# A hybrid MLA and forgetting-attention block: the load of the rotary queries moved behind the mask biases in the sync queue, and half of the first rotary stores moved one stage later

## The chip, the cores and the metric

The kernel runs on one core of a Trainium2 chip. The metric is the device time of one execution in microseconds; lower is better. Three executions of the kernel before gave 579.85 us as the median (579.05 to 580.62).

A core has a matrix engine (TensorE: PE, and PEld for its weight loads), VectorE (DVE), ScalarE (ACT), GpSimd (POOL) and a sync engine (SP). In this kernel every DMA is issued by SP. SP takes its instructions one after the other, so a DMA that has to wait for something keeps all later ones waiting behind it.

## The reference

One decoder layer on 512 real tokens and 16 learned tokens ahead of them, model width 1024. A combined projection of the normalised input feeds two attention branches of 16 heads each and the gates. MLA is the branch with low-rank queries and keys and rotary positions (scores have a 64-wide part and a 32-wide rotary part). FoX is the forgetting attention: its scores get a bias from cumulated log forget gates, one row per head.

```
(cq, ckv, k_pe_raw, z_mla, fq, fk, fv, f_logit, z_fox, gate_a, gate_b) = split(u @ w_in)
q  = rmsnorm(cq) @ w_uq      # per head: 64 plain + 32 rotary columns
kv = rmsnorm(ckv) @ w_ukv    # per head: 64 key + 64 value columns
o_mla = softmax(causal(q_m k_m^T * MLA_SCALE)) v_mla             # q_m, k_m = plain part and rope(rotary part)
o_fox = softmax(causal(fq fk^T * FOX_SCALE + cum_t - cum_s)) fv  # cum = cumsum(log_sigmoid(f_logit + b))
mixed = (sigmoid(gate_a) * ((o_mla * silu(z_mla)) @ w_br_mla)
       + sigmoid(gate_b) * ((o_fox * silu(z_fox)) @ w_br_fox)) @ w_out
out = x + rmsnorm(mixed)
```

Only the 512 real tokens are returned.

## The kernel before

Everything is kept transposed: features on the 128 partitions, tokens along the free dimension. Products are made in parts (a high and a low half of weights and activations, three matmuls for one), so that TensorE's fast types give nearly float32 results.

**Stages.** Attention runs in 16 stages, two heads (a pair) each: `stages = [(br, pr) ...]` with `br` 1 for FoX, 0 for MLA, and `pr` the pair. Stage 0 is FoX pair 0, stage 1 MLA pair 0, stage 2 FoX pair 1, and so on; an even stage is FoX, an odd one MLA. The loop over `si` writes one stage as: `sc()`, the two heads' scores (`st`), their eviction by VectorE (L979: scale, add the bias, row minimum) and the exponentials on ScalarE; `late`, which is the last stage's `values` (`ov`: probabilities times values); then a `fill` of projections for the stages to come (`z`, `mq`, `mk`, `v` in an FoX stage; `fq`, `fk`, `v` in an MLA stage), with `n0` and `n1` in between, which normalise the probabilities into `pn` (L1050 on ScalarE, L1054 on VectorE, small pieces on GpSimd at L1035 to L1040) and send them through DMA transposes into `pt`, five in a stage (6, 10, 14, 10 and 8 tiles). So `ov` of stage n stands on TensorE right behind `st` of stage n+1, and needs the transposes of stage n. TensorE runs in the order in which the program is written (`manual_schedule`).

**Weights in stages.** The loads `wraw` are 512 KB pieces of `w_in`. ScalarE or VectorE finds their peak (`junk` L201, `sc` L203), a tiny matmul `scale` spreads it over the partitions, ScalarE makes the high half (L258), and GpSimd (L271, L272) or VectorE (L269) the low half. A buffer of `wraw` is free for the next load when its low half is made. In an MLA stage three of them are loaded, two for the gates `z` of the next FoX stage: their `scale` matmul stands in the middle of the `v` matmuls of that same MLA stage.

**Rotary queries.** They are made for eight heads at once (`pe_unit`), 0 to 7 in the beginning and 8 to 15 in stages 5 to 9, and stored to `qpe_dram` (`store`: two DMAs for one of the halves `x` = 0 or 1, from `gT0` or `gT1`). `load_qp(pr)` reads one pair's back as `QP`, 256 KB; the MLA scores of pair `pr` read `QP` (stage 2 pr + 1). `QP` has one buffer, free when the MLA scores of the pair before are done. The load is called in `q_done`, when the projection `mq` of stage 2 pr is written.

**Mask biases.** `bias(pr)` loads the two heads' rows of cumulated gates (`cbp`, 264 KB each) from `c_dram`; `masked_bias` makes the causal copy on GpSimd (`cbm`). Their buffers are free when VectorE has evicted the FoX scores.

**Order of SP's queue.** A scheduler sets it from the order in which the program is written, what each DMA depends on and its estimates of time; `tc.issue_after(ins)` puts what is written under it behind `ins` on the same engine, and `keep_in_program_order` holds the stores in the order written. The queue therefore need not follow the text.

Of the kernel before, what the change touches and what calls it, by code (L numbers as in the profile page):

```python
# [26 lines left out]
NH = 16  # L27
# [24 lines left out]
def f32(ap):  # L52
    return ap.bitcast(F32)
# [3 lines left out]
def block_kernel(ctx: ExitStack, tc: tile.TileContext, x, meta_tokens, pre_norm_g, w_in, fox_forget_b,  # L57
# [303 lines left out]
    def run(steps):  # L361
        for _, fn in steps:
            fn()
# [359 lines left out]
    with ExitStack() as att:  # L723
# [38 lines left out]
        nc.gpsimd.memset(vh[:, 0], 0.0)  # L762
        for b in range(4):
            nc.gpsimd.memset(pn[b // 3][:, PN_STEP * b % 15], 0.0)
        gT = []
        masks, normed, whole, turned_p, between = [], [], [], [], []

        wuqh = wuq.rearrange("p k (h e) -> p k h e", e=NOPE + ROPE)
# [1 line left out]
        def load_qp(pr):  # L770
            dma(f32(QP), qpe_dram[2 * pr : 2 * pr + 2].rearrange("h i x f s -> (h i x f) s"))

        def q_mla(pr):
            ld = []

            def load():
                if not ld:
                    ld.append(wload([wuq[:, :, 192 * pr : 192 * pr + 192], wukv[:, 256 * pr : 256 * pr + 256]], mla_room))

            def get():  # L780
                load()
                u, raw, _, _ = ld[0]
                wh, wl = half_rooms(u)
                cuts = [(raw[:, 0:384].rearrange("p (b e) -> p b e", e=96)[:, :, 0:NOPE], lambda t: t[:, 0:256].rearrange("p (b e) -> p b e", e=NOPE)),
                        (raw[:, 384:640].rearrange("p (h a e) -> p a h e", h=2, a=2), lambda t: t[:, 256:512].rearrange("p (a h e) -> p a h e", a=2, h=2))]
                for src, to in cuts:
                    with tc.issue_after(behind[0]) if behind else nullcontext():
                        nc.scalar.copy(to(wh), src)
                for src, to in cuts:
                    split_lo(nc.gpsimd, to(wl), src, to(wh))  # L790
                w = mw[pr] = [(wh[:, o : o + 128], wl[:, o : o + 128]) for o in range(0, 512, 128)]
                return (lambda k: w[k][0]), (lambda k: w[k][1])
            get.load = load

            halves = hl_done(("q", 0, pr), S, S)

            def q_done(i, ps):
                halves(i, ps)
                if pr:
                    load_qp(pr)  # L800
            return unit(f"mq{pr}", get, cq_act, 2, REAL, q_done)


# [289 lines left out]

            return scores, norm(0), norm(1), values

        def stores(a, b):

            written[0] = True
            for x in range(2):
                store0(x, a, b)  # L1100
            written[0] = False

        def bias(pr):

            return [nc.sync.dma_start(cb[0][h], c_dram[2 * pr + h : 2 * pr + h + 1].broadcast_to([128, L])).ins
                    for h in range(2)][1:]
# [33 lines left out]
        pe0, rest0, store0, both0 = pe_unit(0)  # L1140
# [41 lines left out]
        for si, (br, pr) in enumerate(stages):  # L1182
            last = si + 1 == len(stages)
# [66 lines left out]
        for si, (br, pr) in enumerate(stages):  # L1250
            last = si + 1 == len(stages)
            sc, n0, n1, va = attention(br, pr)

            fill = fills[si]
            sc()
            for fn in late:
                fn()
            if si == 0:
# [24 lines left out]
            else:  # L1283
# [2 lines left out]
                run(fill[:3])  # L1286
                if si == 3:
                    with tc.issue_after(turned_p[0]):
                        stores(4, 8)
                run(fill[3:5])  # L1290
                if si == 1:

# [1 line left out]
                if si == 2:  # L1294
                    behind.clear()
                n0()
                if pr and not (br or last):
                    bias(pr + 1)
                if br:
                    sets[si][0].scale()  # L1300
                for job in middles[si]:
# [22 lines left out]
                            peaks(sets[si + 1][1:2], nc.vector)  # L1324
                if not (br or last):
                    masked_bias()
                if 6 <= si < 8:

                    written[0] = True
                    rest1(si - 6)  # L1330
                    written[0] = False
# [382 lines left out]
```

## Time and profile before

| | |
|---|---|
| median of three executions | 579.85 us (579.05 to 580.62) |
| the profiled execution | 580.09 us |
| span of its instructions | 578.3 us |
| TensorE busy | 563.0 us, 97% of the span |
| VectorE, ScalarE, GpSimd busy | 467.3, 390.4, 232.0 us |
| DMA: moved, share of 16 engines' span | 97.74 MB, 71.8% |
| granted TensorE clock | 0.999 |

The profile tells of one execution. Its rows give, for each instruction or run of alike instructions, the start and the length in microseconds, the engine, the line and the tiles (out<-in); in square brackets stands how long the engine was idle before, and who ended that. On the queue of SP (`SPq`) a row is the issuing of DMAs, not the transfer. The chain of waits follows the last instruction back through what released it; there a row with DMA begins at the issue and ends when the data has landed.

### The profile page before, as it was taken

How to read it: one execution, taken by the hardware profiler on the slowest of the kernel's cores; microseconds unless marked ns; L12 is line 12 of the kernel's file. 1: busy time of each engine (PE TensorE's matmuls, PEld its weight loads, DVE VectorE, ACT ScalarE, POOL GpSimd, SP SyncE). 2: the span in 40 equal slices, each digit the busy share in tenths (PEclk: the TensorE clock that was granted, in tenths of full speed). 3: DMA queues.
4: the chain of work that ended last, by engine and by line, in shares of the span. 5: the costliest groups of instructions: out<-in, count | busy, mean ns of one | idle time of the engine just before them, and what ended most of it. 6: DMA issues, size and time to landing. Idle time of an engine off the chain costs nothing.

```text
span 578.3 us, 11369 instructions
## 1 busy us (share of the span) xinstructions
PE 563.0 (97%) x3864; PEld 401.1 (69%) x3864; DVE 467.3 (81%) x1251; ACT 390.4 (68%) x859; POOL 232.0 (40%) x346
## 2 busy tenths in 40 slices
PE   8999989999999999999999999999999999999995
PEld 7888657667668567667666676545686675788884
DVE  5868799878878989868878788879958986478966
ACT  6858688887895886877877878864443463343762
POOL 4331823775695597746837856600000000000000
PEclk9999999999999999999999999999999999999999
DMA  8425999889999897997999987659823230333603
GB/s 282 108 74 153 244 169 294 191 196 244 198 247 191 160 202 123 227 216 152 233 234 186 214 182 144 156 99 297 284 74 109 74 111 10 107 103 109 219 0 145
DMA packets 220537, 97.74 MB, mean 169 GB/s; under 512 B 131864, under 2 KB 210080, under 8 KB 220480
## 3 DMA queue, kind: packets, MB, share of 16 engines
q1 hardware_dynamic: 220480, 97.03, 71.8%
q8 instruction: 30, 0.49, 0.3%
q14 instruction: 27, 0.22, 0.1%
HBM read 62.62 MB, written 4.23 MB: 116 GB/s over the span
## 4 chain that ended last, share of the span: by engine, by line
PE 69%; DVE 9%; ACT 3%; DMA 2%; issue 1%; DVEq 0%; POOL 0%; ACTq 0%; POOLq 0%
PE z L104 15%; PE pg L104 10%; PE py L104 8%; PE x L104 6%; PE v L104 6%; PE st L104 5%; PE fk L104 5%; PE fq L104 5%; PE ov L104 4%; PE mq L104 2%; PE y L104 2%; DMA wraw<-in_w_in_dram 1%; DVE sc L203 1%; DVE w L269 1%; DVE wl L110 1%
## 5 line engine op out<-in xcount | busy, mean ns | idle before, releaser
L104 PEld LDWEIGHTS <-w 128*128 128x128 f16 x1584 | 149.9, 98 | 114.8 <-issue 3.9
L1014 ACT ACTIVATE sf<-sf,nb 128x272 f32<-128x272 f32 (+3 forms) x128 | 72.7, 569 | 25.3 <-DVE nb L979 23.1
L104 PE MATMUL z<-hTh,w 128*128 128x512 f16 x256 | 81.9, 380 | 0.0
L272 POOL TENSOR_TENSOR w<-wraw,w 128x1024 f16<-128x1024 f32 x35 | 74.9, 2141 | 2.3
L104 PE MATMUL pg<-hTh,w 128*128 128x512 f16 x240 | 72.6, 379 | 0.7 <-DVE w L269 0.7
L1054 DVE SCALAR_TENSOR_TENSOR pn<-sf,ri,pn 128x512 f16<-128x512 f32 (+3 forms) x128 | 70.8, 611 | 1.5 <-ACT pn L1050 1.5
L219 POOL TENSOR_SCALAR sc<-sc,su 128x2 f32<-128x2 f32 (+2 forms) x22 | 8.3, 378 | 147.4 <-DVE sc L216 147.4
L258 ACT ACTIVATE w<-wraw,sc 128x1024 f16<-128x1024 f32 x43 | 48.3, 1144 | 24.6 <-DVE sc L218 18.9
L1050 ACT ACTIVATE pn<-sf,ri 128x128 f16<-128x128 f32 (+3 forms) x128 | 59.5, 547 | 0.5 <-DVE ri L1020 0.5
L104 PE MATMUL z<-hTl,w 128*128 128x512 f16 x128 | 48.5, 379 | 0.0
L110 DVE TENSOR_TENSOR wl<-wraw,w 128x512 fp32r<-128x512 f32 (+1 forms) x44 | 38.5, 882 | 12.2 <-PE scale L104 4.4
L271 POOL TENSOR_SCALAR wraw<-wraw,sc 128x1024 f32<-128x1024 f32 x35 | 39.7, 1134 | 19.8 <-ACT w L258 19.8
L104 PE MATMUL pg<-hTl,w 128*128 128x512 f16 x120 | 45.5, 379 | 0.0
L104 PE MATMUL st<-hlk,hlq 64*128 64x272 f32 (+4 forms) x480 | 41.8, 299 | 0.3 <-DVE hlk L387 0.2
L104 PE MATMUL fk<-hTh,w 128*128 128x272 f16 (+1 forms) x224 | 40.1, 276 | 0.0
L104 PE MATMUL v<-hTh,w 128*128 128x272 f16 (+1 forms) x224 | 39.4, 276 | 0.0
L104 PEld LDWEIGHTS st<-hlk,hlq 64*128 64x128 f32 x480 | 33.1, 186 | 6.5 <-ACT vh L903 2.5
L104 PE MATMUL ov<-pt,vp 128*64 128x512 f16 (+4 forms) x416 | 32.7, 307 | 3.1 <-DMA pt<-pn 2.9
L104 PE MATMUL fq<-hTh,w 128*128 128x512 f16 x112 | 34.5, 380 | 0.0
L104 PEld LDWEIGHTS <-vp 128*64 128x64 f16 (+1 forms) x416 | 21.9, 109 | 16.0 <-issue 7.4
L1417 ACT CAST w<-wraw 128x512 fp32r<-128x512 f32 x28 | 16.8, 617 | 23.1 <-DVE wraw L1426 18.6
L165 ACT CAST w<-wraw 128x1024 fp32r<-128x1024 f32 (+1 forms) x20 | 20.2, 1014 | 17.0 <-PE py L104 15.3
(342 smaller groups left out, 1481.0 us busy)
## 6 DMA issues: line engine op xcount, KB each, us to landing
wraw<-in_w_in_dram SPq DMA_DIRECT2D x47, 512.0 KB
room<-in_w_in_dram SPq DMA_DIRECT2D x9, 512.0 KB
cbp<-c_dram SPq DMA_DIRECT2D x16, 264.0 KB
wraw<-in_w_br_fox_dram SPq DMA_DIRECT2D x8, 512.0 KB
tb<-in_w_out_dram SPq DMA_DIRECT2D x8, 512.0 KB
wraw<-in_w_br_mla_dram SPq DMA_DIRECT2D x8, 512.0 KB
wraw<-in_w_out_dram SPq DMA_DIRECT2D x6, 512.0 KB
QP<-qpe_dram SPq DMA_DIRECT2D x8, 256.0 KB
```

Source lines behind the costliest of these rows:

```text
L104: nc.tensor.matmul(*a, **k)
L110: return eng.tensor_tensor(out=lo, in0=src, in1=f32(hi), op=ALU.subtract)
L165: nc.scalar.copy(wh[:, :n], raw[:, :n])
L203: tc.keep_in_program_order(nc.vector.tensor_reduce(out=mp, in_=raw, op=ALU.max, axis=AX.X, apply_absolute_value=True))
L219: nc.gpsimd.tensor_scalar(out=r, in0=t, scalar1=su[:, 5:6], scalar2=1.0, op0=ALU.mult, op1=ALU.mult)
L258: self.hi = nc.scalar.activation(hi, raw, AF.Copy, scale=self.s).ins
L271: nc.gpsimd.tensor_scalar(out=raw, in0=raw, scalar1=self.s, scalar2=1.0, op0=ALU.mult, op1=ALU.mult)
L272: nc.gpsimd.tensor_tensor(out=lo, in0=raw, in1=hi, op=ALU.subtract)
L1014: exps[b // 3] = nc.scalar.activation(sf, sf, AF.Exp, bias=sums["nb"][:, h, b : b + 1], scale=-1.0, accum_out=sums["su"][:, h, b : b + 1]).ins
L1050: normed[:] = [nc.scalar.activation(hi, sf, AF.Copy, scale=rib).ins]
L1054: nc.vector.scalar_tensor_tensor(out=lo, in0=sf, scalar=rib, in1=hi, op0=ALU.mult, op1=ALU.subtract)
L1417: nc.scalar.copy(to[0], src)
```

## The change

Four edits. `q_done` issues the load of the rotary queries behind the second mask bias, where one was asked for in this stage. The mask biases of pair pr + 1 are asked for in the FoX stage of pair pr right behind its scores (pairs 1 to 6) and no longer in the MLA stage behind `n0`. `stores` writes one half `x`. In stage 3 the half x = 0 of the stores for heads 4 to 7 stays behind the transposes of stage 2, and the half x = 1 moves behind those of stage 3.

```diff
             def q_done(i, ps):
                 halves(i, ps)
                 if pr:
-                    load_qp(pr)
+                    with tc.issue_after(biased[0]) if biased else nullcontext():
+                        load_qp(pr)
+                    biased.clear()
...
-        def stores(a, b):
+        def stores(x, a, b):
 
             written[0] = True
-            for x in range(2):
-                store0(x, a, b)
+            store0(x, a, b)
             written[0] = False
...
             fill = fills[si]
             sc()
+            if br and 1 <= pr < NH // 2 - 1:
+                biased[:] = bias(pr + 1)
             for fn in late:
...
                 if si == 3:
                     with tc.issue_after(turned_p[0]):
-                        stores(4, 8)
+                        stores(0, 4, 8)
...
                 n0()
-                if pr and not (br or last):
-                    bias(pr + 1)
                 if br:
...
                 if not (br or last):
                     masked_bias()
+                if si == 3:
+                    with tc.issue_after(turned_p[0]):
+                        stores(1, 4, 8)
```

On TensorE, VectorE, ScalarE and GpSimd the order of the instructions stays as it was. On SP the mask biases keep their places too; six of the eight loads of `QP`, two stores and one weight load move.

SP's queue around the beginning of stage 8 (FoX pair 4), before. `gT_1000` is `gT1`, the source of the half x = 1; `wraw` are weight loads, `vp<-vh` the transpose of the values.

```order
L98 DMA_TRANSPOSE pt<-pn_757 128x8x128
L98 DMA qpe_dram<-gT_1000 2x16x512 x2
L98 DMA QP<-qpe_dram 128x512
L98 DMA wraw_4160<-in_w_in_dram 128x8x128
L98 DMA wraw_4162<-in_w_in_dram 128x8x128
L98 DMA_TRANSPOSE vp_761<-vh 128x9x128
L1105 DMA cbp_746<-c_dram 128x528
L1105 DMA cbp_745<-c_dram 128x528
L98 DMA_TRANSPOSE pt<-pn_756 128x6x128
```

The same place now:

```order
L98 DMA_TRANSPOSE pt<-pn_757 128x8x128
L98 DMA qpe_dram<-gT_1000 2x16x512 x2
L98 DMA wraw_4162<-in_w_in_dram 128x8x128
L98 DMA wraw_4164<-in_w_in_dram 128x8x128
L98 DMA_TRANSPOSE vp_761<-vh 128x9x128
L1106 DMA cbp_746<-c_dram 128x528
L1106 DMA cbp_745<-c_dram 128x528
L98 DMA QP<-qpe_dram 128x512
L98 DMA_TRANSPOSE pt<-pn_756 128x6x128
```

The load of `QP` passed two weight loads, one transpose of values and the two mask biases, and stands now right ahead of the stage's transposes of probabilities. Stage 10 changes in the same way, there behind two stores of 6x16x512. For pairs 1, 2, 3 and 6 (stages 2, 4, 6 and 12) the load comes from the stage before, where it stood ahead of the odd stage's transposes (for pair 1 ahead of one more weight load); those of pairs 0 and 7 stay.

SP's queue at the beginning of stage 3 (MLA pair 1), before:

```order
L98 DMA_TRANSPOSE pt<-pn_757 128x8x128
L98 DMA qpe_dram<-gT_999 4x16x512 x2
L98 DMA qpe_dram<-gT_1000 4x16x512 x2
L98 DMA wraw_1924<-in_w_in_dram 128x8x128
L98 DMA wraw_2195<-in_w_uq_dram 128x2x192
L98 DMA wraw_2195<-in_w_ukv_dram 128x256
L98 DMA wraw_2355<-in_w_in_dram 128x8x128
L98 DMA_TRANSPOSE vp_760<-vh 128x9x128
L98 DMA wraw_2357<-in_w_in_dram 128x8x128
L98 DMA QP<-qpe_dram 128x512
L98 DMA_TRANSPOSE pt<-pn_756 128x6x128
```

and now, from behind the two stores from `gT0` (`gT_999`) to the end of the stage:

```order
L98 DMA wraw_1922<-in_w_in_dram 128x8x128
L98 DMA wraw_2197<-in_w_uq_dram 128x2x192
L98 DMA wraw_2197<-in_w_ukv_dram 128x256
L98 DMA wraw_2357<-in_w_in_dram 128x8x128
L98 DMA wraw_2359<-in_w_in_dram 128x8x128
L98 DMA_TRANSPOSE vp_760<-vh 128x9x128
L98 DMA_TRANSPOSE pt<-pn_756 128x6x128
L98 DMA_TRANSPOSE pt<-pn_757 128x10x128
L98 DMA_TRANSPOSE pt<-pn_756 128x10x128
L98 DMA_TRANSPOSE pt<-pn_756 128x14x128
L98 DMA_TRANSPOSE pt<-pn_757 128x8x128
L98 DMA qpe_dram<-gT_1000 4x16x512 x2
```

The two stores from `gT1` and the load of `QP` left the place ahead of the transposes, and the second weight load stands now ahead of the values' transpose.

More of the change, by code (lines that the diff above doesn't have):

```diff
@@ L764, in block_kernel @@
             nc.gpsimd.memset(pn[b // 3][:, PN_STEP * b % 15], 0.0)
-        gT = []
+        gT, biased = [], []
         masks, normed, whole, turned_p, between = [], [], [], [], []
```

## The prediction

> **What bounds the kernel now.** I read the page first, then the busy times of four pairs of stages side by side, then TensorE in time where those differ, and last the queue of SP.
>
> ```profile
> span 578.3 us, 11369 instructions
> PE 563.0 (97%) x3864; PEld 401.1 (69%) x3864; DVE 467.3 (81%) x1251; ACT 390.4 (68%) x859; POOL 232.0 (40%) x346
> ```
>
> TensorE is busy for all but 15 us of the span. No matmul is removed by the change, so it can gain only where TensorE waits. The next view has the engines' busy time from one FoX `st` to the next, for stages 6+7, 8+9, 10+11 and 12+13 (length, then PE, PEld, DVE, ACT, POOL, granted clock, DMA share, GB/s).
>
> ```profile
> 186.79:225.94 39.15, 39.15 (x323) 26.74 (x322) 35.32 (x112) 30.96 (x73) 29.65 (x42) 1.00 0.89 173
> 225.94:266.33 40.39, 39.40 (x323) 27.00 (x322) 32.03 (x112) 31.04 (x73) 25.86 (x39) 1.00 0.96 197
> 266.33:307.07 40.74, 39.32 (x322) 26.95 (x322) 32.58 (x113) 31.42 (x74) 28.04 (x40) 1.00 1.00 204
> 307.07:346.23 39.16, 39.16 (x322) 26.75 (x322) 32.43 (x113) 31.28 (x73) 25.96 (x38) 1.00 0.93 197
> ```
>
> The four pairs do the same matmuls. Two take 39.15 and 39.16 us with TensorE busy throughout: that is the floor of a pair. Stages 8+9 take 1.23 us more (40.39 - 39.16), stages 10+11 1.58 us more (40.74 - 39.16). The granted clock is 1.00 in all. What TensorE waited for there, and once more in stage 4, the engine's rows in time tell:
>
> ```profile
> 144.55 2.26 PE L104 MATMUL st<-hlk,hlq 64*128 64x272 f32 x30
> 146.97 0.62 PE L104 MATMUL ov<-pt,vp 80*64 80x512 f16 x4 [0.16 <-PE st L104]
> 259.51 0.16 PE L104 MATMUL scale<-sc,spread 128*128 128x2 bf16 x1 [0.98 <-ACT junk L201]
> 288.82 2.13 PE L104 MATMUL ov<-pt,vp 80*64 80x512 f16 x26 [1.42 <-DMA pt<-pn]
> ```
>
> At 259.51 the spreading of the gates' peaks is late, since ScalarE's peak is late; at 288.82 the probabilities' transposes are late. Both come from SP's queue:
>
> ```profile
> 250.47 7.75 DMA wraw<-in_w_in_dram
> 284.55 4.19 DMA pt<-pn
> ```
>
> These are from the chain of waits: a weight load issued at 250.47 lands at 258.22, and a transpose issued at 284.55 lands at 288.74, 0.08 us ahead of the matmul. Now SP's queue ahead of them, with the wait that stands out in it and the DMA engines' share in that wait:
>
> ```profile
> 224.63 1.28 SPq L98 DMA_DIRECT2D qpe_dram<-gT  x2
> 230.05 0.35 SPq L98 DMA_DIRECT2D QP<-qpe_dram  x1
> 230.50 1.00 SPq L98 DMA_DIRECT2D wraw<-in_w_in_dram  x2
> ...
> 235.53 1.00 SPq L1105 DMA_DIRECT2D cbp<-c_dram  x2
> 236.63 9.64 SPq L98 DMA_TRANSPOSE pt<-pn  x5
> ...
> 248.01 5.54 SPq L98 DMA_DIRECT2D wraw<-in_w_in_dram  x3
> ...
> 266.43 1.48 SPq L98 DMA_DIRECT2D qpe_dram<-gT  x2
> 272.37 0.35 SPq L98 DMA_DIRECT2D QP<-qpe_dram  x1
> 272.83 1.00 SPq L98 DMA_DIRECT2D wraw<-in_w_in_dram  x2
> ...
> 279.43 8.69 SPq L98 DMA_TRANSPOSE pt<-pn  x5
> ```
>
> ```profile
> SPq L98 <- DMA qpe_dram<-gT: 8.5, 2, 4.4
> 227.00:231.00 4.00, 4.00 (x47) 2.61 (x44) 3.93 (x27) 2.83 (x9) 3.92 (x4) 1.00 0.11 39
> 268.00:272.40 4.40, 4.40 (x42) 2.44 (x39) 4.29 (x31) 3.84 (x13) 4.22 (x6) 1.00 0.30 91
> ```
>
> In stages 8 and 10 the load of QP stands right behind the stores that write what it reads. SP holds from 225.91 (224.63 + 1.28) to 230.05, 4.14 us, and from 267.91 to 272.37, 4.46 us, while the DMA engines are busy 0.11 and 0.30 of the time, against 0.96 and 1.00 over the two pairs. Everything late in these two pairs is queued behind that hold.
>
> **The change part by part.** It adds no instruction and removes none.
>
> *Stages 8 and 9.* The load of QP goes behind the mask biases. It still needs the two stores, but is reached some eight microseconds after their issue, by when (230.05) they had landed. Who is next behind the stores? The two weight loads, which need buffers that GpSimd frees, and then the transposes, which need GpSimd's pieces of `pn`:
>
> ```profile
> 227.84 2.13 POOL L272 TENSOR_TENSOR w<-wraw,w 128x1024 f16<-128x1024 f32 x1
> 235.07 0.40 POOL L1039 TENSOR_TENSOR pn<-mt,pn 128x96 f16<-128x96 f32 x1
> 268.42 2.13 POOL L272 TENSOR_TENSOR w<-wraw,w 128x1024 f16<-128x1024 f32 x1
> 275.45 0.40 POOL L1039 TENSOR_TENSOR pn<-mt,pn 128x96 f16<-128x96 f32 x1
> ```
>
> So the second weight load goes out not before 229.97 and the first transpose not before 235.47, against some 231 and 236.63. On SP that is 1.0 to 1.2 us. On the DMA engines it is more: the weight loads start on engines that are idle now, so up to the 4.1 us of the hold. The loads of stage 9 (248.01) queue behind these transposes. How much earlier must the last one land? ScalarE's rows say:
>
> ```profile
> 256.60 1.06 ACT L201 ACTIVATE junk<-wraw 128x1024 bf16<-128x1024 f32 x1 [2.50 <-DMA wraw<-in_w_in_dram]
> 258.31 1.06 ACT L201 ACTIVATE junk<-wraw 128x1024 bf16<-128x1024 f32 x1 [0.56 <-DMA wraw<-in_w_in_dram]
> ```
>
> ScalarE stood idle for 2.50 us for the first piece and 0.56 us for the second. With both pieces 1.2 us earlier the wait of TensorE is gone. Gain: 1.0 (only SP's part) to 1.23 us (all that the pair loses); I take 1.2, since the DMA engines' idle time is the larger part.
>
> *Stages 10 and 11.* The same hold, and more room: second weight load not before 270.55 (268.42 + 2.13) against about 273.3, first transpose not before 275.85 against 279.43. That is 2.7 to 3.6 us on SP, and the wait is 1.42 us (1.58 us with the stage's small remainder). Gain 1.58 us; lower bound zero, if the transposes' own time, 8.69 us from first issue to last, were what is late whatever they start from. Stage 12, with the same five, speaks against that: no loss in its pair.
>
> *Stage 3.* Its SP rows, with the next stage's:
>
> ```profile
> 123.59 2.67 SPq L98 DMA_DIRECT2D qpe_dram<-gT  x4
> ...
> 135.05 0.74 SPq L98 DMA_DIRECT2D QP<-qpe_dram  x1
> 135.90 8.68 SPq L98 DMA_TRANSPOSE pt<-pn  x5
> ...
> 152.21 0.87 SPq L1105 DMA_DIRECT2D cbp<-c_dram  x2
> 154.16 8.20 SPq L98 DMA_TRANSPOSE pt<-pn  x5
> ```
>
> Two of four stores (half of 2.67, so 1.3 us of SP) and the load (0.74) leave the place ahead of the transposes: these come up to 2.1 us earlier. `ov` at 146.97 begins 2.42 us after its `st` at 144.55; without a wait that step is 2.19 us (in stage 8 from 225.94, where its pair begins, to 228.13 in the chain of waits). Gain between 0 and 0.24; I take 0.2.
>
> ```profile
> 228.13 1.97 PE ov L104 x26
> ```
>
> *What takes on the moved DMAs.* In stage 4 the stores follow stage 3's transposes: 1.3 us of SP, as much as stage 3 saves. The load of QP comes ahead of the transposes in stages 2, 4, 6 and 12, at 0.35 to 0.74 us of issue. In stage 4 SP is idle from 153.08 to 154.16; the load fits in. In stage 12 as well:
>
> ```profile
> 312.10 0.82 SPq L1105 DMA_DIRECT2D cbp<-c_dram  x2
> 316.61 5.70 SPq L98 DMA_TRANSPOSE pt<-pn  x3
> ```
>
> From 312.92 to 316.61 nothing is issued. I cost these at nothing; the cover is the wait of the transposes for `pn`, and without it 0.4 to 0.7 us in each of four stages would count where no slack is left. And QP itself: behind `cbp` in stage 8 it is issued by 237, against its first use by the `st` of stage 9 at about 243.4. The longest times to landing above are 7.75 us in a crowded queue and 4.19 us for a transpose; at four it is there by 241.
>
> *The mask biases* keep their places in SP's queue: nothing.
>
> **Sum.** 1.2 + 1.58 + 0.2 = 3.0 us. From the profiled execution's 580.09 us that leaves 577.1 (a span of 575.3). It ran 0.24 us over the median of 579.85, so the median to expect is 576.9 us, 0.5% faster. Nothing else that waits is touched: TensorE's other gaps lie ahead of the first moved row or behind the last stage.
>
> **Rivals.** *Half of it.* SP's hold is replaced by the wait for GpSimd's buffers (second load at 229.97), the DMA engines catch up less than I think, and one of the two waits stays: gain 1.2 to 1.8 us, 578.0 to 578.6, median 578.3. For it: in stage 8 SP gains only 1.0 us at the second load. Against it: DMA share 0.11 in the hold.
>
> *No gain.* The transposes and loads are late by the DMA engines' throughput, not by the hold; their share over stages 10+11 is 1.00 (0.93 in 12+13, which lose nothing). Then 579.9.
>
> *Slower: the load ahead of the transposes.* The mechanism sits in stage 4, which gets the two stores and the load of QP, with stage 3 not finishing earlier. Two stores' landing, estimated from the 4.14 us hold for two smaller ones, and the load's 0.74 us make up to 4.9 us ahead of the transposes. Now they are issued by 162.36 (154.16 + 8.20), and `ov` starts at 165.93:
>
> ```profile
> 165.93 1.97 PE ov L104 x26
> ```
>
> In stage 10 issue ended at 288.12, 0.70 us ahead of an `ov` that had waited 1.42; so some 2.1 us are needed, and stage 4 has 3.57 - 2.1 = 1.5 us of slack. Past that it decides: 4.9 - 1.5 = 3.4 us, and if the other stages gain only 1.2 us, 579.85 + 2.2 = 582.1. Against it: stage 3 saves as much queue as stage 4 gets. The Trainium skill ("DMA: Bandwidth & Descriptors", section "Queues, rings and completion order") speaks for this rival: on each DMA engine the descriptors of a queue are taken in ring order, so the transposes cannot overtake the load now ahead of them. By that page's bandwidth of 436 GB/s (its section "Anatomy of one DMA") the 256 KB are an estimated 0.6 us. The rows agree so far as the landing at 258.22 came 7.75 us after issue behind a full queue; no run here shows the load itself in its new place.
>
> **How the numbers follow.** All three gains, or nearly: 0.68, median 576.9, own range 576.0 to 577.9. Half: 0.13. None: 0.10. Slower: 0.09. A measurement tells 0.3%, 1.7 us, from no change. The first case is faster throughout (under 578.1); half (578.3) and none count as the same: 0.23 together. So faster 0.68, same 0.23, slower 0.09. The range for 8 in 10 is 575.8 to 579.3: below it the three executions' scatter of 0.8 us under a full gain, above it half the gain and part of none.
>
> **What would show it.** Right: no row of SP waiting for `qpe_dram<-gT` in the waits; the DMA share in the 4 us behind the stores of stages 8 and 10 well above 0.11 and 0.30; pairs 8+9 and 10+11 at about 39.2 us; `scale` and `ov` there without a bracket; QP in stages 2 to 12 issued behind `cbp`. Wrong: `st` of an MLA stage waiting for QP, or `ov` of stage 5 waiting for `pt`, would be the load or the stores in the wrong place; pairs at 40.4 and 40.7 us with the hold gone would mean that throughput set them. If both pairs reach 39.2 and the time stays, the gain went into the merge behind the last stage.

## The result and the profile after

The changed kernel took 576.58 us (median of 6 executions, 575.57 to 577.77), the kernel before 579.34 us (6, 577.89 to 580.62): ratio 0.9951, 95% interval 0.9933 to 0.997. That is 2.76 us, or 0.5%, faster; the prediction was 576.9 us. The profiled execution took 575.92 us.

The page and the busy times from one FoX `st` to the next, stages 6+7, 8+9, 10+11 and 12+13, then the 4 us right behind the stores of stages 8 and 10 (columns as in the prediction):

```profile
span 574.1 us, 11359 instructions
PE 561.2 (98%) x3864; PEld 398.6 (69%) x3864; DVE 467.6 (81%) x1251; ACT 390.6 (68%) x859; POOL 232.2 (40%) x346
```

```profile
185.36:224.51 39.15, 39.15 (x321) 26.75 (x320) 35.32 (x112) 30.96 (x73) 29.66 (x42) 1.00 0.90 180
224.51:263.67 39.16, 39.16 (x321) 26.72 (x320) 32.47 (x112) 31.28 (x73) 26.97 (x40) 1.00 0.99 205
263.67:302.83 39.16, 39.16 (x321) 26.77 (x320) 32.45 (x112) 31.29 (x73) 26.94 (x39) 1.00 1.06 204
302.83:341.99 39.16, 39.16 (x321) 26.77 (x320) 32.38 (x112) 31.28 (x73) 26.10 (x39) 1.00 0.93 203
...
224.63:228.63 4.00, 4.00 (x56) 3.12 (x56) 3.93 (x24) 2.37 (x8) 3.92 (x4) 1.00 0.68 184
264.72:268.72 4.00, 4.00 (x47) 2.62 (x46) 3.93 (x28) 2.77 (x9) 3.85 (x5) 1.00 0.80 170
```

All four pairs now stand at the floor of 39.16 us with TensorE busy throughout. In the 4 us behind the stores the DMA engines work 0.68 and 0.80 of the time; in the kernel before it was 0.25 and 0.35 from the same place on (225.91 to 229.91 and 267.91 to 271.91; the 0.11 and 0.30 of the prediction are of 227 to 231 and of 268 to 272.4). SP's queue shows why: the load of `QP` is no longer held, and no row of SP's waits names `qpe_dram<-gT` any more.

```profile
223.35 1.28 SPq L98 DMA_DIRECT2D qpe_dram<-gT  x2
225.36 3.69 SPq L98 DMA_DIRECT2D wraw<-in_w_in_dram  x2
229.14 2.04 SPq L98 DMA_TRANSPOSE vp<-vh  x1
231.27 1.02 SPq L1106 DMA_DIRECT2D cbp<-c_dram  x2
232.39 0.37 SPq L98 DMA_DIRECT2D QP<-qpe_dram  x1
234.12 8.72 SPq L98 DMA_TRANSPOSE pt<-pn  x5
...
263.25 1.47 SPq L98 DMA_DIRECT2D qpe_dram<-gT  x2
264.83 2.49 SPq L98 DMA_DIRECT2D wraw<-in_w_in_dram  x2
267.41 5.33 SPq L98 DMA_TRANSPOSE vp<-vh  x1
...
273.94 0.37 SPq L98 DMA_DIRECT2D QP<-qpe_dram  x1
274.41 9.24 SPq L98 DMA_TRANSPOSE pt<-pn  x5
```

Where TensorE had waited, its rows have no bracket now: the `ov` that follows the `st` of stage 4 (2.19 us after 143.41), `scale` of stage 9 (256.92) and `ov` of stage 10 (284.75). (`ov` of a stage stands behind the `st` of the next, so the first is the `ov` of stage 3.) The `ov` at 164.49 is that of stage 4, where the rival saw its wait:

```profile
143.41 2.26 PE L104 MATMUL st<-hlk,hlq 64*128 64x272 f32 x30
145.60 2.04 PE L104 MATMUL ov<-pt,vp 80*64 80x512 f16 x26
...
164.49 1.76 PE L104 MATMUL ov<-pt,vp 80*64 80x512 f16 x18
...
256.92 0.17 PE L104 MATMUL scale<-sc,spread 128*128 128x2 bf16 x1
...
284.75 2.04 PE L104 MATMUL ov<-pt,vp 80*64 80x512 f16 x26
```

The two spans differ by 4.2 us (578.3 - 574.1), more than the medians. Stage by stage, from FoX `st` to FoX `st`, before minus after: opening and stages 0 and 1 +1.25 (104.61 - 103.36), stages 2+3 -0.11, 4+5 +0.22, 6+7 0.00, 8+9 +1.23, 10+11 +1.58, 12+13 0.00, everything behind +0.03. Of the 1.25 us, 1.16 are not the change's: `st` of stage 0, ahead of every moved instruction, began at 62.25 us in the profile of before, at 61.09 us in that of the changed kernel, and between 60.76 and 61.74 us in the second profile of the changed kernel and those of the ten other kernels below, whose instructions are the same up to there. What differs is the start: in the trace of before the record of the full TensorE clock begins at 10.53 us, in the twelve others between 4.88 and 7.64 us, and the eight early matmuls `pt` took 1.97 us there and 1.19 us in the changed kernel. What is left is 2.9 to 3.0 us in the stages that the prediction named.

### The profile page after: what moved, and what is told of

Read it like the earlier page. It is cut to its first block, busy times and chain, and to the rows that moved or that the text cites. A ratio compares the mean times of both kernels' runs of the same rounds, so it can differ in the third digit from the quotient of the medians.

```text
span 574.1 us, 11359 instructions
## 1 busy us (share of the span) xinstructions
PE 561.2 (98%) x3864; PEld 398.6 (69%) x3864; DVE 467.6 (81%) x1251; ACT 390.6 (68%) x859; POOL 232.2 (40%) x346
## 4 chain that ended last, share of the span: by engine, by line
PE 74%; DVE 8%; ACT 2%; issue 1%; DVEq 0%; ACTq 0%
PE z L104 16%; PE pg L104 10%; PE py L104 8%; PE st L104 7%; PE v L104 7%; PE x L104 6%; PE fk L104 6%; PE fq L104 6%; PE ov L104 5%; PE mq L104 2%; PE y L104 2%; DVE sc L203 1%; DVE w L269 1%; DVE wl L110 1%; PE mk L104 1%
```

## The experiments

**The hold alone.** The kernel before, with the load of `QP` at its old place directly behind the stores; for pairs 4 and 5 it reads pair 0's rows, which were written long before. So it leaves out the rotary queries of pairs 4 and 5; the bytes, the order and the place of every DMA are those of before. Only the dependence on the stores ahead is gone.

```diff
-            dma(f32(QP), qpe_dram[2 * pr : 2 * pr + 2]...)
+            src = 0 if pr in (4, 5) else pr
+            with tc.issue_after(last_store[0]) if pr in (4, 5) else nullcontext():
+                dma(f32(QP), qpe_dram[2 * src : 2 * src + 2]...)
```

> The kernel before with one difference: the loads of QP for pairs 4 and 5 stay at their places in SP's queue, right behind the stores, but read the rows of pair 0, written long ago, so that they need not wait for those stores (the rotary part of the scores of pairs 4 and 5 is thereby that of pair 0). Theory (SP's hold until the stores have landed makes stages 8 to 11 late): no row of SP waits for qpe_dram<-gT, the pairs of stages 8+9 and 10+11 take 39.2 us instead of 40.4 and 40.7, and the time falls by 2.8 us against the kernel before (ratio 0.995), without any DMA moved. Rival (what counts is the 256 KB that stand ahead of the weight loads, or the throughput of the DMA engines): the pairs stay at 40.4 and 40.7 us, ratio 1.000.

576.69 us (9 executions, 575.84 to 578.42), ratio 0.9962 (0.9943 to 0.9981). Stages 8+9, 10+11, and SP's queue in stage 8:

```profile
224.77:263.93 39.16, 39.16 (x322) 26.77 (x322) 32.54 (x113) 31.19 (x73) 27.38 (x40) 1.00 1.04 207
263.93:303.09 39.16, 39.16 (x322) 26.75 (x322) 32.43 (x113) 31.27 (x73) 26.45 (x39) 1.00 1.07 209
```

```profile
223.37 1.29 SPq L98 DMA_DIRECT2D qpe_dram<-gT  x2
224.71 1.26 SPq L98 DMA_DIRECT2D QP<-qpe_dram  x1
226.07 3.20 SPq L98 DMA_DIRECT2D wraw<-in_w_in_dram  x2
```

Both pairs reach the floor without a single DMA moved. The load goes out at 224.71, right behind the stores, and the weight loads at 226.07 instead of 230.50. The hold was the cause in both pairs, and throughput was not: the same bytes are moved, at a DMA share of 1.04 and 1.07.

**The two pairs that the prediction costed, and the rest.** First the moved loads for pairs 4 and 5 (stages 8 and 10) without any of the other edits; then the complement, all edits but these.

```diff
-            if br and 1 <= pr < NH // 2 - 1:
+            if br and pr in (4, 5):             # the first; stores as before
+            if br and pr in (1, 2, 3, 6):       # the second; stores split as changed
```

> The kernel before with only the loads of QP for pairs 4 and 5 behind the mask biases; the other loads and the stores as before. Theory: these two places carry nearly the whole gain: pairs 8+9 and 10+11 at 39.2 us, the step from st to ov at the beginning of stage 4 still 2.4 us, time 2.8 us less (ratio 0.995). Rival (the gain comes from all six moved loads and the stores, each a part): about a third, 1 us less, ratio 0.998.

> The changed kernel with the loads of QP for pairs 4 and 5 back at their old places; the loads for pairs 1, 2, 3 and 6 and the stores moved as in the change. Theory: pairs 8+9 and 10+11 at 40.4 and 40.7 us as before, the step from st to ov at the beginning of stage 4 2.19 us instead of 2.42; time 0.2 us less than before, not to be told from none (ratio 0.9996). Rival (each part its share): 2 us less, ratio 0.997. Rival (the moved loads cost something ahead of the transposes of stages 2, 4, 6 and 12, hidden in the sum): up to 1 us more.

The first: 577.42 us (10 executions, 575.72 to 579.47), ratio 0.9971 (0.9951 to 0.999), stages 8+9 and 10+11 both 39.16 us. The second: 578.67 us (10, 576.89 to 579.69), ratio 0.9989 (0.9973 to 1.0005), with the old losses: 40.81 us in stages 8+9 and 40.69 in 10+11, and these rows of SP's waits and of TensorE:

```profile
SPq L98 <- DMA qpe_dram<-gT: 8.6, 2, 4.5
```

```profile
258.99 0.16 PE L104 MATMUL scale<-sc,spread 128*128 128x2 bf16 x1 [0.90 <-ACT junk L201]
...
288.35 1.02 PE L104 MATMUL ov<-pt,vp 80*64 80x512 f16 x7 [1.46 <-DMA pt<-pn]
```

So by the stage times the gain lies in those two of the six moved loads. The times alone say less: by the ratio the first gains 1.7 us of the 2.8 expected. In the second kernel stages 8+9 lose 0.42 us more than in before, and `ov` of stage 8 waits 0.52 us there, at 246.60. One expectation missed: without the split of the stores, stage 4's step from `st` to `ov` was expected to stay at 2.4 us and took 2.19 here, as in the kernel without the hold. What that says of the split is taken up below, where the split alone is undone.

**The split of the stores alone.** The kernel before with two of the first rotary stores moved behind stage 3's transposes. The load for pair 2 now stands right behind them.

```diff
-                        stores(4, 8)
+                        stores(0, 4, 8)
...
+                if si == 3:
+                    with tc.issue_after(turned_p[0]):
+                        stores(1, 4, 8)
```

> The kernel before with only the stores of stage 3 split, the second half at the stage's end. The scheduler puts the load of QP for pair 2 right behind them, so that SP meets a wait for their landing at the beginning of stage 4, as it does in stages 8 and 10. Theory: the step from st to ov at the beginning of stage 4 is 2.19 us (0.2 gained), a new hold of some 4 us shows in SP's waits, of which 1.1 us are covered by SP's idle time ahead of the transposes of stage 4 and about 1.5 us by their slack, so ov at the beginning of stage 5 waits 1 to 2 us; pairs 8+9 and 10+11 stay at 40.4 and 40.7; time 0.8 to 1.8 us more than before (ratio 1.001 to 1.003). Rival (the hold is harmless, position is what counts): time 0.2 us less.

580.31 us (10 executions, 578.24 to 582.33), ratio 1.0013 (0.999 to 1.0037). SP's waits for the stores are three now, and a new wait of TensorE opens, at `ov` of stage 4 (0.65 us, where 1 to 2 were expected):

```profile
SPq L98 <- DMA qpe_dram<-gT: 12.3, 3, 4.2
```

```profile
165.37 0.84 PE L104 MATMUL ov<-pt,vp 80*64 80x512 f16 x6 [0.65 <-DMA pt<-pn]
...
259.98 0.16 PE L104 MATMUL scale<-sc,spread 128*128 128x2 bf16 x1 [1.94 <-ACT junk L201]
```

The split by itself is worth nothing: it makes a third hold. It is of use only with the load moved away. Stages 8+9 took 42.92 us here, 2.53 us more than in before: the wait of `scale` is 0.96 us longer, and the clock fell behind it, as the last section shows. The expectation had 40.7 us for stages 10+11, and they took 39.16, although SP was held in stage 10 as before:

```profile
266.33 1.48 SPq L98 DMA_DIRECT2D qpe_dram<-gT  x2
272.08 0.35 SPq L98 DMA_DIRECT2D QP<-qpe_dram  x1
```

The hold is 4.27 us (from 267.81). But SP issued these stores 2.06 us ahead of TensorE's first `st` of the stage (268.39), since TensorE had lost time in stage 9; in the kernel before it issued them 0.17 us behind (266.43 against 266.26). A hold of this length cost 1.58 us there and nothing here, so what it costs depends on how far the queue is ahead.

**The changed kernel once more.**

> The changed kernel once more, beside the next three. If the first result holds: ratio 0.995 (0.993 to 0.997), all six pairs of stages from stage 4 on at 39.16 us. It tells also whether two things vary between executions of one kernel: the opening ahead of the attention (which ran 1.16 us shorter in the first profile of the changed kernel than in that of before), and the step from st to ov in stage 4 (2.19 us after, 2.42 before). If both come out different here, neither is to be put down to the change.

575.92 us (5 executions, 575.87 to 576.54), ratio 0.995 (0.9935 to 0.9966); the step in stage 4 2.19 us, all pairs behind it 39.16. The result holds.

**The cover of the moved load.** The prediction costed the load ahead of the transposes at nothing, with waits for `pn` as its cover, and had its opposite as a rival. Two kernels add transfers of 256 KB, copies of the pair's rows of `qpe_dram` to a scratch, in the six stages where the load moved: one right behind the load, and then three (two behind the load, the third behind the first transpose). A third kernel has the one extra transfer behind the last transpose of the stage. A copy goes from DRAM to DRAM, in pieces of 16 KB, so it is not quite the load's like. The edits, without the scratch tiles' declaration:

```diff
                         load_qp(pr)
+                        for t in extra[pr] if biased else []:     # one or three scratch tiles
+                            dma(t, qpe_dram[2 * pr : 2 * pr + 2]...)
```

```diff
+                if br and 1 <= pr < NH // 2 - 1:                  # the third: at the end of the stage
+                    with tc.issue_after(turned_p[0]):
+                        for t in extra[pr]:
+                            dma(t, qpe_dram[2 * pr : 2 * pr + 2]...)
```

> The changed kernel with one more transfer of 256 KB (the pair's rows of qpe_dram copied to a scratch in DRAM, in 16 pieces of 16 KB) right behind the moved load of QP, ahead of the transposes, in stages 2, 4, 6, 8, 10 and 12. It doubles what the rival 'slower: the load ahead of the transposes' is made of. If the cover is as the prediction had it (1.5 us of slack in stage 4, several us elsewhere): no gap opens, time as the changed kernel within 0.5 us, 576 to 577. If the cover is thin, as the changed kernel's trace suggests (the transposes' fourth landing stands 0.06 us ahead of ov in stage 4, 0.50 in stage 10, 0.93 in stage 2, over 2 us in stages 8 and 12): ov waits 0.5 to 1.2 us in stage 4 and 0.2 to 0.8 in stage 10, none in 8 and 12, time 577.3 to 578.5.

> The same with three more transfers of 256 KB: two behind the moved load, the third behind the first transpose. Thin cover: each further 256 KB costs about 1 us at the 200 GB/s that these stages move, so ov waits 2 to 3.5 us in stages 2, 4 and 10 and up to 1.5 in stages 6, 8 and 12; time 580 to 586, slower than before: the rival's mechanism is real and one load of 256 KB is just inside the cover. If the transposes' start is set by GpSimd and VectorE (their waits in SP's queue are for pn) and not by what is queued ahead: under 1 us in each, time under 579.

> The same six extra transfers of 256 KB as in the kernel with one more load ahead of the transposes (581.94 us), now behind the last transpose of the same FoX stage, that is at the head of the next MLA stage's queue (ahead of the stores of stages 3, 7 and 9). Same bytes, same number of DMAs, another place in SP's queue. Theory A (the place decides: what stands ahead of the transposes when they are the next thing TensorE needs): the MLA stages' fourth transposes land 1.2 to 5.8 us ahead of ov in the changed kernel, so nothing waits; 576 to 577.5, ratio 0.995 to 0.9975. Theory B (the DMA engines' throughput sets these stages, so that 256 KB cost wherever they stand): as the copy ahead of the transposes, 580.5 to 582, with waits in stages 4 and 10 again.

| six extra transfers of 256 KB each | median, range | ratio to before |
|---|---|---|
| none (the changed kernel, same chip as the next two) | 575.92 us, 575.87 to 576.54 | 0.995 (0.9935 to 0.9966) |
| one, ahead of the transposes | 581.94 us, 580.44 to 585.07 | 1.006 (1.0037 to 1.0084) |
| three, around the first transpose | 587.67 us, 583.82 to 587.96 | 1.0129 (1.0095 to 1.0164) |
| one, behind the transposes | 577.78 us, 576.59 to 579.65 | 0.9966 (0.9949 to 0.9983) |

With one ahead of the transposes, SP's queue in stage 4 and TensorE's rows:

```profile
154.10 0.42 SPq L99 DMA_DIRECT2D QP<-qpe_dram  x1
154.57 0.55 SPq L99 DMA_DIRECT2D extra<-qpe_dram  x1
155.29 10.53 SPq L99 DMA_TRANSPOSE pt<-pn  x5
```

```profile
166.08 1.54 PE L105 MATMUL ov<-pt,vp 80*64 80x512 f16 x14 [1.36 <-issue]
167.87 0.69 PE L105 MATMUL ov<-pt,vp 128*64 128x256 f16 x12 [0.24 <-DMA pt<-pn]
...
288.66 1.54 PE L105 MATMUL ov<-pt,vp 80*64 80x512 f16 x14 [1.76 <-DMA pt<-pn]
291.28 0.69 PE L105 MATMUL ov<-pt,vp 128*64 128x256 f16 x12 [1.08 <-DMA pt<-pn]
```

A second 256 KB is enough to make the kernel slower than before; both theories gave too little, 578.5 at most. The transfer itself is short: in the six stages it landed 0.61 to 0.73 us behind the load ahead of it. Of the six stages it waits in 4 and 10 alone, 43.81 us for stages 4+5 (41.95 in the changed kernel) and 42.26 us for 10+11. In stage 4 SP was late before the extra transfer came: it reached the load of `QP` 10.53 us behind the stage's first `st` (154.10 - 143.57), in the changed kernel 9.41 us (152.82 - 143.41). So part of that stage's loss was there before the transfer; why is open, since with three extra transfers SP reached the load after 9.85 us. With the same bytes behind the transposes TensorE waits once in these stages, in stage 10:

```profile
286.14 1.06 PE L105 MATMUL ov<-pt,vp 80*64 80x512 f16 x8 [0.76 <-DMA pt<-pn]
```

With three, four of the six stages wait (`ov` by 1.46, 2.43, 0.83 and 2.25 us in stages 2, 4, 8 and 10), and the time is above what was expected (580 to 586), in part because the clock fell behind the two longest, as the last section shows.

So the place decides: the same bytes give ratios of 1.006 and 0.9966, with intervals far apart. What they cost behind the transposes is not shown, since that interval overlaps the changed kernel's, and stage 10 waits in one more kernel below that has no extra bytes. The Trainium skill ("DMA: Bandwidth & Descriptors", section "Queues, rings and completion order") has the descriptors of one queue consumed in ring order on each DMA engine, though a later one may finish its write first; this pair of runs agrees with that order, with about 6 us (581.94 - 575.92) for the place ahead, on one chip, and about 1 us by the ratios (0.9966 against 0.995) for the place behind. In stage 4 the extra transfer landed at 160.12 us and the first transpose behind it at 160.87.

How thin is the cover? The trace has the landing of each transpose. The table gives how long the fourth of a stage's five landed ahead of that stage's `ov` (worked out from the trace's completions; below about 0.15 us `ov` was waiting, or just not):

| stage | 2 | 4 | 8 | 10 | 12 |
|---|---|---|---|---|---|
| before | 2.28 | 1.16 | 0.13 | 0.09 (waits 1.42) | 2.24 |
| changed | 0.93 | 0.06 | 2.32 | 0.50 | 2.12 |
| changed, once more | 1.27 | 0.42 | 2.37 | 0.15 | 2.21 |
| extra transfer ahead | 0.56 | 0.09 (waits 1.36) | 1.98 | 0.04 (waits 1.76) | 2.15 |
| extra transfer behind | 1.83 | 1.16 | 1.35 | 0.14 (waits 0.76) | 2.10 |

The two profiles of the changed kernel wait nowhere in these stages, but in stages 4 and 10 they are within half a microsecond of doing so. In the kernel before stage 4 had 1.16 us, so the change left 0.74 to 1.10 us less there.

**The split undone, the loads moved.** The changed kernel with all four first rotary stores behind stage 2's transposes again.

```diff
                         stores(0, 4, 8)
+                        stores(1, 4, 8)
...
-                if si == 3:
-                    with tc.issue_after(turned_p[0]):
-                        stores(1, 4, 8)
```

> The changed kernel without the split of the first rotary stores: all four stand behind stage 2's transposes again, and the moved loads of QP stay. Of the prediction's 3.0 us the split was to bring 0.2, in stage 3. Theory A (the split brings nothing; the step of 2.19 us in stage 4 was reached without it in two earlier kernels, and it takes slack in stage 4, where the fourth transpose lands 0.06 to 0.42 us ahead of ov): time as the changed kernel, ratio 0.995, with about 1 us between landing and ov in stage 4 and about 1 us in stage 3. Theory B (the split is worth its 0.2 us): st to ov in stage 4 takes 2.42 us, time 0.2 us up, which the comparison cannot tell but the trace can. Theory C (with four stores and the next load queued closer, something waits in stage 3 or 4): a gap of over 0.5 us there, 577 to 578.

576.57 us (8 executions, 576.11 to 577.66), ratio 0.9957 (0.9934 to 0.998). The profiled execution has two waits that the changed kernel had not:

```profile
146.62 0.62 PE L104 MATMUL ov<-pt,vp 80*64 80x512 f16 x4 [0.40 <-DMA pt<-pn]
...
286.49 0.84 PE L104 MATMUL ov<-pt,vp 80*64 80x512 f16 x6 [0.67 <-PE st L104]
```

The step at 146.62 took 2.65 us against 2.19: theory B's wait, about twice its size. Stage 3's fourth transpose landed 0.13, 2.19, 0.54 and 0.14 us ahead of `ov` in the four kernels with the stores unsplit (before, the kernel without the hold, the one with pairs 4 and 5 moved, this one), and 3.09 and 3.20 us in the two profiles of the changed kernel. In every profile with the split it landed at least 2.25 us ahead; without it the wait came in two profiles of four. The time cannot tell 0.2 us; that part rests on the traces. The wait in stage 10 goes with SP's lead at the head of that stage: SP issued its stores 0.17 us after TensorE began the stage (264.84 against 264.67), in the changed kernel 0.42 us before it (263.25 against 263.67). It is not handed on from stage 3, since at the head of stage 8 the lead was still 1.38 us, against 1.16 in the changed kernel. What took it in stages 8 and 9 stays open.

**Stores with no load behind them.** The changed kernel, with the first stores of heads 0 to 3 split too: heads 2 and 3 go behind stage 1's transposes.

```diff
-                store(x, 0, 2 if g else 4)
+                store(x, 0, 2)
...
+                if si == 1:
+                    with tc.issue_after(turned_p[0]):
+                        stores(0, 2, 4)
+                        stores(1, 2, 4)
```

> The changed kernel, and the first rotary stores of heads 0 to 3 split like those of heads 4 to 7: heads 0 and 1 stay in stage 0, heads 2 and 3 go behind stage 1's transposes. It asks whether stores that stand close ahead of transposes cost anything where no load waits for them. In the changed kernel ov of stage 0 waits 1.31 us at 85.28 for a transpose; the four stores ahead land between 72.55 and 77.16, each on 5 DMA engines one behind the other, and the load of QP is issued at 77.45, right behind the last landing. Theory A (the stores hold the load, and with it the three transposes behind): with half the bytes they land by about 74 to 75, the load goes out up to 0.7 us earlier, and the gap falls by 0.5 to 0.8 us; ratio 0.9935 to 0.9945 against before. Theory B (the gap is the transposes' own issue time, about 1.9 us each from 74.67 on): gap stays at 1.0 to 1.4 us, ratio as the changed kernel, 0.995.

579.84 us (11 executions, 578.21 to 581.01), ratio 1.0013 (1.0 to 1.0026): the gain is lost. TensorE's rows:

```profile
85.35 1.03 PE L104 MATMUL ov<-pt,vp 80*64 80x512 f16 x7 [0.77 <-DMA pt<-pn]
126.78 0.59 PE L104 MATMUL ov<-pt,vp 80*64 80x512 f16 x3 [0.70 <-DMA pt<-pn]
167.08 2.12 PE L104 MATMUL ov<-pt,vp 80*64 80x512 f16 x23 [1.07 <-DMA pt<-pn]
288.44 0.84 PE L104 MATMUL ov<-pt,vp 80*64 80x512 f16 x6 [0.85 <-DMA pt<-pn]
```

The wait that it aimed at, the first row, was 0.77 us against 1.31 in the changed kernel. Theory A had that, but it is not shown: the kernels whose first stores are unsplit have 0.71 to 1.81 us at that place. The five DMA engines of the expectation are not shown either: in the changed kernel's trace each store's semaphore (the counter that tells of its landing) is raised five times, first 0.4 to 0.7 us after the issue, then four times within half a microsecond, 2.3 to 5.2 us later. Only those four can be landings of the data. With four DMAs more at the head of stage 2, `ov` waits in stages 2, 4 and 10, by 0.70 to 1.07 us. Neither theory had that: the queue in stage 2 has no room for four DMAs, and the delay reaches stage 4, where SP issued the stores at the head 0.51 us ahead of TensorE instead of 1.50. By stage 8 SP had caught up (1.24 us ahead, 1.16 in the changed kernel), so the wait in stage 10 is not shown to come from these stores.

**Relief where the cover is thin.** The changed kernel, with the late stores split once more, so that only what the next load reads stays early.

```diff
-                if si == 3:
+                if 3 <= si < 5:
                     with tc.issue_after(turned_p[0]):
-                        stores(1, 4, 8)
+                        stores(1, 2 * si - 2, 2 * si)
...
-                        store1(si - 8, 2, 8)
+                        store1(si - 8, 2, 8 if si == 8 else 4)
+                if si == 10:
+                    with tc.issue_after(turned_p[0]):
+                        store1(1, 4, 8)
```

> The changed kernel with two more stores split, each so that only what the next load reads stays early: of the half x = 1 of heads 4 to 7, heads 4 and 5 stay behind stage 3's transposes and heads 6 and 7 go behind stage 4's; of the half x = 1 of heads 8 to 15, heads 10 and 11 stay behind stage 9's transposes and heads 12 to 15 go behind stage 10's. It takes bytes from the two FoX stages whose cover the runs so far show to be thinnest (4 and 10) and gives them to MLA stages 5 and 11, where the fourth transpose lands 5.8 and 2.0 us ahead of ov. Theory A (what stands ahead of the transposes in the queue and on the DMA engines is what decides): the fourth transpose lands about 0.5 us or more earlier against ov in stages 4 and 10, no gap opens anywhere from stage 4 on; span as the changed kernel's (574.1) or up to 0.2 us under it, ratio 0.9945 to 0.995. Theory B (the thin cover has another cause, GpSimd's and VectorE's own pace): landings against ov unchanged, 0.1 to 0.5 us, ratio 0.995. If stage 5 or 11 waits instead, 577 and more.

575.95 us (6 executions, 575.36 to 576.53), ratio 0.9933 (0.9914 to 0.9951). In stage 10 SP's queue runs the transposes off like this (in the changed kernel the row is 274.41 and 9.24, against a stage begun 0.29 us earlier):

```profile
273.57 7.91 SPq L98 DMA_TRANSPOSE pt<-pn  x5
```

The fourth transpose lands 2.89 us ahead of `ov` there instead of 0.15 to 0.50, while in stage 4 it lands 0.04 us ahead of it. Theory A holds in stage 10 and fails in stage 4, where half the stores' bytes made no difference. There `ov` even waited 0.19 us there, and stages 4+5 took 42.23 us (41.95 in the changed kernel). Of all kernels tried it has the lowest ratio, but its interval overlaps that of the changed kernel (0.9935 to 0.9966, and 0.9933 to 0.997): faster than before, not shown to be faster than the change.

## Why the prediction was right

**What bounds.** The hold of SP behind the stores was named as the cause of both waits. Taken away by itself it brought the pairs to 39.16 us, so this is shown, not argued. One reading was too sharp: over the whole holds the DMA share was 0.24 and 0.32, not 0.11 and 0.30. And a hold does not cost by itself: in the kernel with only the stores split the one of stage 10 cost nothing, since SP was further ahead of TensorE.

**Stages 8 and 9, 1.2 us.** Measured 1.23 (40.39 - 39.16). The steps on the way came out too: the second weight load went out at 228.68 and the first transpose at 234.12. Stage 8 began 1.36 us earlier than before (224.51 against 225.87), so in the time of before that is 230.04 and 235.48, for a predicted 229.97 and 235.47. (225.87 is the first `st` itself; the 225.94 of the prediction is 0.07 us into it.) The weight load that the chain of waits had from 250.47 to 258.22 now lands at 254.58, which is 2.3 us earlier in that time: more than the 1.2 us that were needed, as the prediction had it of the DMA engines' idle time.

**Stages 10 and 11, 1.58 us.** Measured 1.58 (40.74 - 39.16). Here the way there was less exact. The transposes were to come 2.7 to 3.6 us earlier on SP; they came 2.43 us earlier (274.41 + 2.59, the lead at that stage, is 277.00 for 279.43 before), since the transpose of the values held SP for 5.33 us (4.31 before). The wait of 1.42 us was covered with 0.50 us to spare, and 0.15 in the second profile, not with one or two.

**Stage 3, 0.2 us.** Measured 0.22 over stages 4+5 and 0.23 in the step. As a single figure it is good; it stands for a wait that is 0 to 0.46 us without the split, by execution.

**The base.** The sum was taken from a profiled execution whose opening was the slowest of all those profiled; the span fell by 4.2 us and not by 3.0. The medians do not carry this: 2.76 us against 3.0, with an interval of 1.7 to 3.9 us, so it is the stage times that bear out the three terms. That 576.9 came within 0.3 us of the measured 576.58 is in part luck: the median of before was 0.51 us lower in six executions than in three, and the gain 0.24 us smaller.

**What was costed at nothing** cost nothing, but the reason given for it was too generous. The prediction found 1.5 us of slack in stage 4; by the landing it was 1.16 us, and the changed kernel has 0.06 to 0.42 us of it left. The extra 256 KB, ahead of the transposes, cost 1.86 us in stages 4+5 (43.81 - 41.95). The prediction had an estimated 0.6 us for such a load, from the bandwidth of 436 GB/s of the Trainium skill ("DMA: Bandwidth & Descriptors", section "Anatomy of one DMA"), which that section states for DMAs issued by GpSimd. As the time of the transfer that was near (0.61 to 0.73 us). As the price for TensorE it was not, and why TensorE lost more is shown only in part: SP was 1.1 us late in that stage before the transfer came. The number that misled was the "2.1 us needed" from issue to `ov`: in the changed kernel issue ends 0.98 us ahead of `ov` in stage 4 (153.41 + 10.10 = 163.51, against 164.49) and nothing waits. What `ov` waited for was the fourth transpose in each wait of the table, and here the fifth landed 0.95 us behind the start of `ov`.

**The rivals.** "Half of it" did not happen. "No gain", by throughput, is refuted by the kernel without the hold and by the extra bytes behind the transposes. "Slower: the load ahead of the transposes" names a real mechanism, in stage 4 and also in stage 10, which it did not name and which lost more with the extra transfer (3.10 us against 1.86). One load is just inside the cover, a load and a copy are outside, and the kernel is then slower than before: its chance of 0.09 was on the low side.

## What to carry to other kernels

A DMA that reads what the DMA just ahead of it writes holds the whole queue until that has landed, here over 4 us; whether that costs time depends on how far the queue is ahead of the engine that it feeds. Look for it as a low DMA share at a place where the queue is waiting, and put independent DMAs in between. Before something is moved ahead of transposes or loads that are needed soon, take the time from the landing of the needed one to its first use, stage by stage: an average DMA share or the time from issue does not show whether half a microsecond is left or three. Where a queue has little room, a delay is handed on: DMAs added in stage 2 opened waits in stages 2 and 4.

## What the runs showed of the hardware that was not expected

A wait of TensorE of about 2 us was enough to halve its granted clock. It happened in the kernel with only the stores split, behind the wait of 1.94 us at 259.98, and in the one with three extra transfers, behind one of 2.43 us at 168.31 (and one of 2.25 us at 295.29). For each of the first two, the stretch with the wait and the next one:

```profile
256.82:260.23 3.41, 1.47 (x14) 1.10 (x13) 0.00 (x0) 1.75 (x5) 0.00 (x0) 1.00 0.76 180
260.23:263.64 3.41, 3.41 (x18) 2.35 (x16) 3.07 (x7) 1.17 (x3) 0.27 (x1) 0.50 1.08 211
```

```profile
168.31 2.00 PE L105 MATMUL ov<-pt,vp 80*64 80x512 f16 x16 [2.43 <-DMA pt<-pn]
```

```profile
166.05:169.47 3.42, 1.16 (x12) 0.86 (x14) 2.12 (x13) 3.27 (x12) 2.96 (x7) 1.00 1.08 216
169.47:172.88 3.41, 3.41 (x23) 2.02 (x19) 1.86 (x6) 2.23 (x5) 2.22 (x7) 0.50 1.07 311
```

Waits up to 1.81 us left the clock at 1.00. One is the wait of 1.76 us at 288.66 above, with a second one of 1.08 us behind it:

```profile
285.00:288.41 3.41, 1.90 (x26) 1.56 (x24) 3.41 (x20) 2.90 (x11) 3.03 (x3) 1.00 1.10 208
288.41:291.82 3.41, 2.08 (x26) 1.33 (x26) 0.86 (x5) 2.41 (x7) 2.08 (x8) 1.00 1.19 171
```

With the clock at 0.50 the 36 matmuls of `v` behind 259.98 took 5.70 us instead of 4.03, so the wait cost nearly twice its length. The Trainium skill ("TensorE: Matmul & The Clock Gate", section "What's actually happening") has the clock halved after at least one idle window of about 3.4 us; here it was halved after 1.94 us. The traces tell more than the length of a wait. In all thirteen (one of each kernel here, two of the changed one) the granted clock changes only at whole multiples of 3.413 us from where its record begins: at 260.23 and 263.64 in the first kernel (74 and 75 times, from 7.64), at 169.47 and 172.88 in the second (48 and 49 times, from 5.62). The rows above are cut at such places. Half clock followed every stretch of the grid in which TensorE ran no matmul for 1.94 us or more, and none with 1.84 us or less; in between lies no case. The ends of the traces show that it is the grid, and not the length alone. In the kernel with the split undone the clock halved 2.51 us behind TensorE's last matmul (572.36 against 569.85), at the next place of the grid. In the one with one extra transfer ahead the next place came 1.84 us behind it (575.12 against 573.28) and the clock stayed at 1.00 until the place after that, 5.25 us behind it (578.53). Behind the two waits that the change removed, 0.98 and 1.42 us, the clock stayed at 1.00.
